# Hybrid encoder step on one core: the S5 lift set between its gates, the SSD beside the other gates

## Chip, cores and metric

One core of a Trainium2 chip runs the whole program. The metric is the device time of one execution in microseconds (us). The engines are called PE (TensorE, with its weight loads PEld), DVE (VectorE), ACT (ScalarE), POOL (GpSimd) and SP (SyncE, which issues every DMA of this kernel).

## What is computed

One layer of a hybrid encoder on 592 rows (16 meta tokens, 512 prompt rows, 64 sample rows) of width 1024. All is float32.

```
h = rmsnorm(x)
p = h @ w_in                       # columns z, xbc, dt, u, q, k, v, gates
y_a = groupnorm(ssd(xbc, dt) * silu(z))         # Mamba-2 scan in chunks
y_b = s5(u)                                     # complex diagonal scan
glu = gelu(y_b) @ w_glu
out_b = glu[:, :1024] * sigmoid(glu[:, 1024:])
o_c = stick_breaking(q, k, v)                   # with a cache of 512 rows
g0, g1, g2 = sigmoid(h @ w_gate)                # three gates of width 1024
mix = g0*(y_a @ w_lift_a) + g1*out_b + g2*(o_c @ w_lift_c)
x = x + mix @ w_out
x = x + relu(rmsnorm(x) @ w_up)**2 @ w_down
```

## The kernel before

Everything is kept transposed, channels on partitions, rows along the free axis. Each weight block of 128x1024 numbers is a *unit*; `units` (L71) lists them in the order in which they are loaded and used: u, then q, v and k, then `mixed()` (L62: ten xbc, eight z, then the gates g1, g2, g0 with eight units each), then eight glu, four lc, eight la, eight out, and the MLP. A float32 product is made of three passes: weights and operands are split into a high and a low part (`split`, L252, ACT writes the high, DVE the low part), and `mm3` (L331) issues hi*hi, hi*lo and lo*hi for each block of 128 rows of the contraction.

`dense` (L379) runs one unit over two halves of the columns (288 each). A half of a gate unit is 24 matmuls (eight blocks); glu and lc contract over 512 channels only, so a half there is 12 matmuls and one unit has two outputs. Each half has one PSUM tile `ps_d` out of three (L190), which is free again when its reader is done. In a glu unit (L1466) ACT turns the second output into `gls` by a sigmoid, DVE multiplies it into the gate `gt`, and DVE multiplies the first output with that into `mix`. In a gate unit (`do_gate`, L552) ACT's sigmoid alone empties the PSUM tile, and the gate goes to DRAM (`g_scr`). A gate is loaded back by `gate_tile` (L1450) into one of three `gt` tiles. For lc, DVE multiplies the output with g2 and POOL adds it to `mix`.

The three branches between the projections are Python generators. After each half, `side` (L373) adds the branch's number in `PACE` (L35) to a credit, and for each whole credit `pull` runs the generator to its next `yield`; so S5, attention and SSD lie between the dense halves, one after the other. `in_order` keeps a pulled piece behind what its engines were given before; a scheduler then fixes each engine's order.

At the end of S5 its output goes to DRAM (`yb_scr`); attention loads it back tile by tile (`s5_load`, L873) and splits it into `ybx` (`s5_split`, L878), one of four tiles in each of its four rounds. The SSD works through six chunks. Behind them `gated` (L1345) multiplies with z and gathers squares in `sa` (part 0 are the first 288 columns, part 1 the others, two channel tiles at a time), `normed` (L1359) sums `sa` over partitions with a matmul by ones (`ps_n`, L408), takes the reciprocal root (`rstd_of`, L240: Ln, Exp and Square on ACT, two steps on DVE) and multiplies four channel tiles of `ya`; `scaled_split` makes `yah` and `yal` for la. Before, part 1 is gated whole, then both groups are normed, each followed by its four splits:

```python
            for m in range(0, 8, 2):
                gated(1, m)
                yield
            for g in range(2):
                normed(1, g)
                yield
                for m in range(4 * g, 4 * g + 4):
                    scaled_split(ya[:, m, on], sg[:, m:m + 1], yah[:, m, on], yal[:, m, on])
```

glu starts behind `until("attn")`, la behind `until("gated")`.

Of the kernel before, what the change touches and what calls it, by code (L numbers as in the profile page):

```python
# [17 lines left out]
T = TP + TS  # L18
# [16 lines left out]
PACE = {"s5_parts": 1.25, "s5": 1.35, "attention": 1.8, "ssd": 1.1}  # L35
# [26 lines left out]
def mixed():  # L62
    n = dict.fromkeys("xzabc", 0)
    out = []
    for c in ORDER:
        out.append(({"x": "xbc", "z": "z", "a": "g1", "b": "g2", "c": "g0"}[c], n[c]))
        n[c] += 1
    return out


def units():  # L71
    u = [("u", m) for m in range(4)] + [(n, m) for m in range(4) for n in ("q", "v", "k")]
    u += mixed()
    u += [("glu", m) for m in range(8)] + [("lc", m) for m in range(4)]
# [102 lines left out]
def body(tc, io):  # L177
# [6 lines left out]
    with ExitStack() as ctx:  # L184
# [303 lines left out]
        oc_scr = dram.tile([8, 128, T], F32, name="oc_scr")  # L488
        g_scr = [dram.tile([8, 128, T], F32, name="g_scr%d" % j) for j in range(3)]
# [62 lines left out]
        def do_gate(j, m):  # L552
            o = etile("go", "ec")
            dense(("g%d" % j, m), hh, hl, lambda cols, ps: sigmoid(ps, o[:, cols]))
            SP.dma_start(g_scr[j][m, :, on], o[:, on])
# [164 lines left out]
        def s5():  # L720
# [150 lines left out]
            yield  # L871

# [12 lines left out]
        def attention():  # L885
# [100 lines left out]
            for t in range(4):  # L986
                (v, vc), (kc, ks, qs) = vv, new
                yb = s5_load(t)
# [139 lines left out]
                s5_split(t, yb)  # L1128
                yield
            a1.release()  # L1130
            ap.release()
            done["attn"] = True
# [71 lines left out]
        def ssd():  # L1204
# [160 lines left out]
            for c in range(1, 6):  # L1365
# [3 lines left out]
                if c == 5:  # L1369
                    normed(0, 0)  # L1370
# [15 lines left out]
                if c == 5:  # L1386
                    normed(0, 1)
# [5 lines left out]
                if c == 4:  # L1393
                    gated(0, 4)
                    gated(0, 6)
                yield
# [7 lines left out]
            for m in range(0, 8, 2):  # L1404
                gated(1, m)
                yield
            for g in range(2):
                normed(1, g)
                yield
                for m in range(4 * g, 4 * g + 4):  # L1410
                    scaled_split(ya[:, m, on], sg[:, m:m + 1], yah[:, m, on], yal[:, m, on])
                    if m % 2:
                        yield
# [16 lines left out]
        pulls.append((attention(), PACE["attention"]))  # L1430
        for n, m in mixed():
# [4 lines left out]
            elif n == "z":  # L1436
                do_z(m)
            else:
                do_gate(int(n[1]), m)

        def until(n):
            while n not in done:
                pull()


        until("s5")
        lp, ybx = late["p"], late["ybx"]
# [8 lines left out]
        ocx = keep.tile([128, 8, T], F32R, name="ocx", tag="hh")  # L1456
        for m in range(8):
            g = gate_tile(1, m)
            s = etile("gls", "ec")

            def ev_b(cols, ps):
                sigmoid(ps, s[:, cols])
# [199 lines left out]
```

## Time and profile before

| | |
|---|---|
| Median of the runs | 1118.86 us (1118.25, 1118.86, 1122.1) |
| Profiled execution, its own time | 1120.97 us |
| Its span | 1119.2 us |
| Mean granted clock, of full speed | 0.994 |
| PE busy, matmuls | 1100.5 us (98%), 8532 |
| PEld busy | 1061.7 us (95%) |
| DVE busy | 794.3 us (71%) |
| ACT busy | 539.6 us (48%) |
| POOL busy | 183.7 us (16%) |
| DMA | 144.04 MB, mean 129 GB/s |

A busy PE isn't a PE at its peak: matmuls overlap, so the number of matmuls in a stretch tells more than its busy time. The stages, from the tiles' first and last instructions: S5 ends at 283 us, the gates run from 291 to 511 us with attention beside them (294 to 482), the SSD from 482 to 584 us, glu from 510 to 598, lc from 598 to 628, la from 628 to 680.

### The profile page before, as it was taken

To read this page: it belongs to the slowest core of one execution; us is meant where nothing else is said; L and a number is where in the kernel's file an instruction comes from. 1 tells how busy PE (TensorE), PEld (TensorE's weight loads), DVE (VectorE), ACT (ScalarE), POOL (GpSimd) and SP (SyncE) were. 2 spreads that over 40 slices of the span, in tenths; PEclk is the share of its full clock that TensorE was granted. 3 is DMA by queue.
4 is the path that set the end of the run, shared out by engine and by line. 5 is a ranking of instruction groups with operands and counts; after the bars stand their busy time and mean duration, and the time that the engine had idled before them with its cause. 6 is when DMAs were issued, how large, how long until landed. Compare 5 with 4: busy or idle time off the path is not lost.

```text
span 1119.2 us, 21309 instructions
## 1 busy us (share of the span) xinstructions
PE 1100.5 (98%) x8532; PEld 1061.7 (95%) x8532; DVE 794.3 (71%) x1377; ACT 539.6 (48%) x896; POOL 183.7 (16%) x240
## 2 busy tenths in 40 slices
PE   9999999999999999999998999999999999999998
PEld 8998999999998999898788999999999999999998
DVE  7968579955667475549988754467866785786787
ACT  6455465523365455465668323355444444444443
POOL 2086256611000000005422300300000000000000
PEclk9999999989999999999999999999999999999999
DMA  7663224466754353277445543322232223223222
GB/s 275 147 145 115 84 90 125 110 165 165 241 177 138 113 179 133 89 255 257 129 146 167 151 134 99 99 75 94 76 102 88 75 77 115 74 76 129 79 81 80
DMA packets 80594, 144.04 MB, mean 129 GB/s; under 512 B 26512, under 2 KB 40688, under 8 KB 79984
## 3 DMA queue, kind: packets, MB, share of 16 engines
q1 hardware_dynamic: 80496, 142.69, 41.0%
q8 instruction: 67, 1.10, 0.4%
q14 instruction: 31, 0.25, 0.1%
HBM read 117.40 MB, written 24.38 MB: 127 GB/s over the span
## 4 chain that ended last, share of the span: by engine, by line
PE 80%; DVE 10%; POOL 3%; ACT 2%; DMA 2%; issue 2%; SPq 1%; DVEq 0%; ACTq 0%; POOLq 0%
PE ps_d L336 18%; PE ps_d L337 18%; PE ps_d L338 18%; PE ps_x L1581 3%; PE ps_x L1580 3%; PE ps_x L1582 3%; PE ps_o L895 2%; PE ps_z L895 2%; PE ps_y L1581 1%; PE ps_y L1580 1%; PE ps_y L1582 1%; DVE w_lo L217 1%; DVE ar L1272 1%; DVE ar L217 1%; POOL cm L217 1%
## 5 line engine op out<-in xcount | busy, mean ns | idle before, releaser
L336 PE MATMUL ps_d<-hh,w_hi 128*128 128x288 f32 (+1 forms) x864 | 260.5, 301 | 0.0
L338 PE MATMUL ps_d<-hh,w_lo 128*128 128x288 f32 (+1 forms) x864 | 260.0, 301 | 0.0
L337 PE MATMUL ps_d<-hl,w_hi 128*128 128x288 f32 (+1 forms) x864 | 260.0, 301 | 0.0
L253 ACT ACTIVATE w_hi<-w_raw 128x1024 fp32r<-128x1024 f32 (+1 forms) x150 | 151.8, 1012 | 220.7 <-PE ps_d L337 142.8
L217 DVE TENSOR_TENSOR w_lo<-w_raw,w_hi 128x1024 fp32r<-128x1024 f32 (+1 forms) x150 | 179.2, 1195 | 104.2 <-ACT w_hi L253 103.7
L337 PEld LDWEIGHTS ps_d<-hl,w_hi 128*128 128x128 f32 x864 | 164.5, 190 | 0.9 <-issue 0.3
L338 PEld LDWEIGHTS ps_d<-hh,w_lo 128*128 128x128 f32 x864 | 164.7, 191 | 0.5
L336 PEld LDWEIGHTS ps_d<-hh,w_hi 128*128 128x128 f32 x864 | 164.7, 191 | 0.4
L336 PE MATMUL ps_d<-x2h,w_hi 128*128 128x288 f32 x512 | 151.3, 296 | 0.0
L337 PE MATMUL ps_d<-x2l,w_hi 128*128 128x288 f32 x512 | 151.1, 295 | 0.0
L338 PE MATMUL ps_d<-x2h,w_lo 128*128 128x288 f32 x512 | 150.3, 295 | 0.0
L338 PEld LDWEIGHTS ps_d<-x2h,w_lo 128*128 128x128 f32 x512 | 96.2, 188 | 0.1
L336 PEld LDWEIGHTS ps_d<-x2h,w_hi 128*128 128x128 f32 x512 | 96.2, 188 | 0.1
L337 PEld LDWEIGHTS ps_d<-x2l,w_hi 128*128 128x128 f32 x512 | 96.2, 188 | 0.0
L253 ACT ACTIVATE w_hi<-ws 128x1024 fp32r<-128x1024 f32 x32 | 34.0, 1061 | 55.0 <-PE ps_y L1581 21.7
L1581 PE MATMUL ps_x<-ftl,w_hi 128*128 128x288 f32 x192 | 56.7, 295 | 0.5 <-DVE ftl L217 0.5
L1580 PE MATMUL ps_x<-fth,w_hi 128*128 128x288 f32 x192 | 56.8, 296 | 0.2 <-ACT s L1600 0.2
L1582 PE MATMUL ps_x<-fth,w_lo 128*128 128x288 f32 x192 | 56.4, 294 | 0.0
L1531 ACT ACTIVATE fr<-ps_d 128x288 f32<-128x288 f32 x64 | 25.7, 402 | 55.8 <-PE ps_d L338 55.8
L217 POOL TENSOR_TENSOR xe<-xd,tend 128x1024 f32<-128x1024 f32 (+2 forms) x6 | 11.6, 1942 | 234.4 <-DVE xd L217 210.1
L217 DVE TENSOR_TENSOR w_lo<-ws,w_hi 128x1024 fp32r<-128x1024 f32 x32 | 39.0, 1220 | 12.6 <-ACT w_hi L253 12.6
L906 DVE TENSOR_TENSOR_SCAN aw<-col,aw 128x400 f32<-128x400 f32 (+4 forms) x36 | 30.7, 899 | 17.3 <-ACT aw L250 17.2
(472 smaller groups left out, 2727.1 us busy)
## 6 DMA issues: line engine op xcount, KB each, us to landing
w_raw<-wts SPq DMA_DIRECT2D x150, 512.0 KB, 3.5
g_scr<-go SPq DMA_DIRECT2D x24, 288.0 KB, 2.8
gt<-g_scr SPq DMA_DIRECT2D x24, 288.0 KB, 3.1
ar<-ac_scr SPq DMA_DIRECT2D x4, 1024.0 KB, 7.2
x_scr<-cs SPq DMA_DIRECT2D x10, 297.5 KB, 2.9
xc<-x_scr SPq DMA_DIRECT2D x4, 640.0 KB, 7.0
xt<-xT SPq DMA_DIRECT2D x8, 296.0 KB, 5.7
z_scr<-zs SPq DMA_DIRECT2D x8, 288.0 KB, 4.6
```

What stands on the lines that cost most here:

```text
L217: e.tensor_tensor(o, a, b, op=op)
L253: S.activation(hi, x, AF.Copy)
L336: PE.matmul(ps, wh[:, c], xh[:, k, cols], start=start and k == 0, stop=False)
L337: PE.matmul(ps, wh[:, c], xl[:, k, cols], start=False, stop=False)
L338: PE.matmul(ps, wl[:, c], xh[:, k, cols], start=False, stop=stop and k == kt - 1)
L895: mm = lambda *a, **b: PE.matmul(*a, skip_group_check=True, **b)
L906: V.tensor_tensor_scan(x, one.to_broadcast([128, n]), x, 1.0, op0=OP.mult, op1=OP.mult)
L1272: V.tensor_scalar(ar[:n, h, :n], ar[:n, h, :n], acm[:n, c, h:h + 1], 0.0, op0=OP.subtract, op1=OP.min)
L1531: S.activation(r[:, cols], ps, AF.Relu)
L1580: PE.matmul(ps, w[0][:, o], fh[:, k], start=first and k == 0, stop=False, skip_group_check=True)
L1581: PE.matmul(ps, w[0][:, o], fl[:, k], start=False, stop=False, skip_group_check=True)
L1582: PE.matmul(ps, w[1][:, o], fh[:, k], start=False, stop=k == 3, skip_group_check=True)
```

## The change

The eight glu units stand between the g1 gates (g1 0, glu 0, g1 1, ...). The g1 gate stays in its SBUF tile, is multiplied there, and the product goes to DRAM (`m_scr`) in the place of the gate; it is loaded into `mix` before lc uses it. `ybx` is needed for that before g1 starts, so S5's own generator loads and splits it, and the main loop pulls until that is done. The attention's output `ocx` takes `ybx`'s place and is loaded when attention ends. g2 and g0 follow, with the SSD's number in `PACE` at 1.25 in place of 1.1. In the SSD's tail the steps of part 0 move by one, and part 1 goes gated 0, 2, 4, normed 0, gated 6, two pieces of splits, normed 1, two pieces of splits.

```diff
--- before.py
+++ after.py
@@ -32,7 +32,7 @@
 LEAD = 120
 WARM = 14
 SPLITS = 3
-PACE = {"s5_parts": 1.25, "s5": 1.35, "attention": 1.8, "ssd": 1.1}
+PACE = {"s5_parts": 1.25, "s5": 1.35, "attention": 1.8, "ssd": 1.25}
 BUFS = {"ea": 3, "eb": 4, "ec": 3}
 
@@ -64,6 +64,8 @@
     out = []
     for c in ORDER:
         out.append(({"x": "xbc", "z": "z", "a": "g1", "b": "g2", "c": "g0"}[c], n[c]))
+        if c == "a":
+            out.append(("glu", n[c]))
         n[c] += 1
     return out
 
@@ -71,7 +73,7 @@
 def units():
     u = [("u", m) for m in range(4)] + [(n, m) for m in range(4) for n in ("q", "v", "k")]
     u += mixed()
-    u += [("glu", m) for m in range(8)] + [("lc", m) for m in range(4)]
+    u += [("lc", m) for m in range(4)]
     u += [("la", m) for m in range(8)] + [("out", m) for m in range(8)]
 
     up = [[("up", 8 * b + 4 * j + k) for k in range(4) for j in range(2)] for b in range(4)]
@@ -486,6 +488,7 @@
         yb_scr = dram.tile([512, 8 * NY], F32, name="yb_scr")
         ya_scr = dram.tile([8, 128, T], F32, name="ya_scr")
         oc_scr = dram.tile([8, 128, T], F32, name="oc_scr")
+        m_scr = dram.tile([8, 128, T], F32, name="m_scr")
         g_scr = [dram.tile([8, 128, T], F32, name="g_scr%d" % j) for j in range(3)]
         ac_scr = dram.tile([96, 128], F32, name="ac_scr")
 
@@ -552,7 +555,24 @@
         def do_gate(j, m):
             o = etile("go", "ec")
             dense(("g%d" % j, m), hh, hl, lambda cols, ps: sigmoid(ps, o[:, cols]))
-            SP.dma_start(g_scr[j][m, :, on], o[:, on])
+            if j != 1:
+                SP.dma_start(g_scr[j][m, :, on], o[:, on])
+            return o
+
+        def do_glu(m, g):
+
+            ybx = late["ybx"]
+            s = etile("gls", "ec")
+
+            def ev_b(cols, ps):
+                sigmoid(ps, s[:, cols])
+                tt(V, g[:, cols], g[:, cols], s[:, cols], OP.mult)
+
+            def ev_a(cols, ps):
+                tt(V, g[:, cols], ps, g[:, cols], OP.mult)
+            w = dense(("glu", m), ybx[:, 0:4], ybx[:, 4:8], ev_b, kt=4, base=4)
+            dense(None, ybx[:, 0:4], ybx[:, 4:8], ev_a, kt=4, base=0, w=w)
+            SP.dma_start(m_scr[m, :, on], g[:, on])
 
         def do_xbc(m):
             pre = etile("pre", "ea", XW)
@@ -869,6 +889,12 @@
             late["dt"] = tc.alloc_tile_pool(name="dtp", bufs=1)
             done["s5"] = True
             yield
+            for m in range(4):
+                x = s5_load(m)
+                yield
+                s5_split(m, x)
+            done["ybx"] = True
+            yield
 
         def s5_load(m):
             x = late["p"].tile([128, T], F32, name="ybl", tag="gt%d" % (m % 3))[:, :8 * NY]
@@ -985,7 +1011,6 @@
             yield
             for t in range(4):
                 (v, vc), (kc, ks, qs) = vv, new
-                yb = s5_load(t)
                 q2, kh, kl = [], [], []
                 for h in range(2):
                     kd, qd = kq[h]
@@ -1125,10 +1150,12 @@
                 split(po[:, 0:TS], och[:, 512:], ocl[:, 512:])
                 SP.dma_start(oc_scr[t, :, on], och.bitcast(F32))
                 SP.dma_start(oc_scr[4 + t, :, on], ocl.bitcast(F32))
-                s5_split(t, yb)
                 yield
             a1.release()
             ap.release()
+            late["ocx"] = ocx = late["p"].tile([128, 8, T], F32R, name="ocx", tag="ybx")
+            for j in range(8):
+                SP.dma_start(ocx[:, j, on].bitcast(F32), oc_scr[j, :, on])
             done["attn"] = True
 
 
@@ -1366,8 +1393,6 @@
                 if c < 5:
                     turned(c + 1)
                 weigh(c)
-                if c == 5:
-                    normed(0, 0)
                 yield
                 if c < 5:
                     decay(c + 1)
@@ -1384,7 +1409,7 @@
                 else:
                     st = sn
                 if c == 5:
-                    normed(0, 1)
+                    normed(0, 0)
                 fetch_chunk(c + 2)
                 yield
                 if c < 5:
@@ -1393,6 +1418,8 @@
                 if c == 4:
                     gated(0, 4)
                     gated(0, 6)
+                if c == 5:
+                    normed(0, 1)
                 yield
             SP.dma_start(io["ssd_out"][1], st)
             d2.release()
@@ -1401,16 +1428,14 @@
             late["l2"] = l2 = tc.alloc_tile_pool(name="late2", bufs=1)
             late["yah"] = yah = l2.tile([128, 8, T], F32R, name="yah", tag="yah")
             late["yal"] = yal = l2.tile([128, 8, T], F32R, name="yal", tag="yal")
-            for m in range(0, 8, 2):
-                gated(1, m)
-                yield
-            for g in range(2):
-                normed(1, g)
-                yield
-                for m in range(4 * g, 4 * g + 4):
+            def parted(m0):
+                for m in range(m0, m0 + 2):
                     scaled_split(ya[:, m, on], sg[:, m:m + 1], yah[:, m, on], yal[:, m, on])
-                    if m % 2:
-                        yield
+
+            for f, x in ((gated, (1, 0)), (gated, (1, 2)), (gated, (1, 4)), (normed, (1, 0)), (gated, (1, 6)),
+                         (parted, (0,)), (parted, (2,)), (normed, (1, 1)), (parted, (4,)), (parted, (6,))):
+                f(*x)
+                yield
             done["gated"] = True
 
 
@@ -1428,6 +1453,10 @@
             do_v(m)
             do_qk("k", m, kg, io["k_out"], halves)
         pulls.append((attention(), PACE["attention"]))
+        def until(n):
+            while n not in done:
+                pull()
+
         for n, m in mixed():
             if n == "xbc":
                 do_xbc(m)
@@ -1435,16 +1464,17 @@
                     pulls.append((ssd(), PACE["ssd"]))
             elif n == "z":
                 do_z(m)
+            elif n == "g1":
+                if m == 0:
+                    until("ybx")
+                g1 = do_gate(1, m)
+            elif n == "glu":
+                do_glu(m, g1)
             else:
                 do_gate(int(n[1]), m)
 
-        def until(n):
-            while n not in done:
-                pull()
-
-
-        until("s5")
-        lp, ybx = late["p"], late["ybx"]
+
+        lp = late["p"]
         mix = keep.tile([128, 8, T], F32, name="mix", tag="hl")
 
         def gate_tile(j, m):
@@ -1453,27 +1483,13 @@
             return g
 
         until("attn")
-        ocx = keep.tile([128, 8, T], F32R, name="ocx", tag="hh")
-        for m in range(8):
-            g = gate_tile(1, m)
-            s = etile("gls", "ec")
-
-            def ev_b(cols, ps):
-                sigmoid(ps, s[:, cols])
-                tt(V, g[:, cols], g[:, cols], s[:, cols], OP.mult)
-
-            def ev_a(cols, ps):
-                tt(V, mix[:, m, cols], ps, g[:, cols], OP.mult)
-            w = dense(("glu", m), ybx[:, 0:4], ybx[:, 4:8], ev_b, kt=4, base=4)
-            dense(None, ybx[:, 0:4], ybx[:, 4:8], ev_a, kt=4, base=0, w=w)
-            if m >= 4:
-                for j in (m - 4, m):
-                    SP.dma_start(ocx[:, j, on].bitcast(F32), oc_scr[j, :, on])
+        ocx = late["ocx"]
         for m2 in range(4):
             w = None
             for j in range(2):
                 m = 2 * m2 + j
                 g = gate_tile(2, m)
+                SP.dma_start(mix[:, m, on], m_scr[m, :, on])
 
                 def ev_c(cols, ps):
                     tt(V, g[:, cols], ps, g[:, cols], OP.mult)
```

How the instructions stand on three places. First ACT at the end of S5; `gsq` is S5's last activation, `zs` a z unit's sigmoid, `go` that of a gate, `ybx<-ybl` the split of S5's output. Before:

```order
L855 ACTIVATE gsq<-ps_y_3234 128x292
L250 ACTIVATE gsq<-gsq 128x292
L253 ACTIVATE w_hi<-w_raw 128x1024
L250 ACTIVATE zs<-ps_d 128x288 x2
L253 ACTIVATE w_hi<-w_raw 128x1024
L250 ACTIVATE zs<-ps_d 128x288
L250 ACTIVATE go<-ps_d 128x288
L253 ACTIVATE w_hi<-w_raw 128x1024
L250 ACTIVATE go<-ps_d 128x288
```

After the change, from the third of the four loads on:

```order
L255 ACTIVATE ybx<-ybl 128x512
L255 ACTIVATE ybx<-ybl 128x64
L252 ACTIVATE zs<-ps_d 128x288
L255 ACTIVATE w_hi<-w_raw 128x1024
L252 ACTIVATE zs<-ps_d 128x288
L255 ACTIVATE ybx<-ybl 128x512
L255 ACTIVATE ybx<-ybl 128x64
L252 ACTIVATE go<-ps_d 128x288
L255 ACTIVATE w_hi<-w_raw 128x1024
L252 ACTIVATE go<-ps_d 128x288
L252 ACTIVATE gls<-ps_d 128x288 x2
```

The splits stand ahead of the first g1 gate, the fourth directly, and two sigmoids of glu 0 follow that gate.

Second, PE where lc (`ocx`) ends and la (`yah`, `yal`) starts. Before, the last `ps_n` stands inside lc, 132 matmuls ahead of la, here:

```order
L337 MATMUL ps_d_7510<-ocx_6889,w_hi_7368 128x288
L338 MATMUL ps_d_7510<-ocx_6889,w_lo_7369 128x288
L408 MATMUL ps_n_6807<-sa_5576,ones_89 128x288
L336 MATMUL ps_d_7524<-ocx_6889,w_hi_7368 128x288
L337 MATMUL ps_d_7524<-ocx_6889,w_hi_7368 128x288
L338 MATMUL ps_d_7524<-ocx_6889,w_lo_7369 128x288
```

and the passage to la is plain:

```order
L336 MATMUL ps_d_7691<-ocx_6889,w_hi_7504 128x288
L337 MATMUL ps_d_7691<-ocx_6889,w_hi_7504 128x288
L338 MATMUL ps_d_7691<-ocx_6889,w_lo_7505 128x288
L336 MATMUL ps_d_7716<-yah_6567,w_hi_7572 128x288
L337 MATMUL ps_d_7716<-yal_6568,w_hi_7572 128x288
L338 MATMUL ps_d_7716<-yah_6567,w_lo_7573 128x288
L336 MATMUL ps_d_7716<-yah_6567,w_hi_7572 128x288
```

After the change the last `ps_n` stands between the two:

```order
L338 MATMUL ps_d_7684<-ocx_5417,w_hi_7492 128x288
L339 MATMUL ps_d_7684<-ocx_5417,w_hi_7492 128x288
L340 MATMUL ps_d_7684<-ocx_5417,w_lo_7493 128x288
L410 MATMUL ps_n_6891<-sa_5702,ones_89 128x288
L338 MATMUL ps_d_7709<-yah_6651,w_hi_7562 128x288
L339 MATMUL ps_d_7709<-yal_6652,w_hi_7562 128x288
```

and three halves of la (ps_d_7709, 7735, 7772) first take their four blocks of channel tiles 0 to 3, 36 matmuls in all, and then tile 4 in turns:

```order
L339 MATMUL ps_d_7772<-yal_6652,w_hi_7632 128x288
L340 MATMUL ps_d_7772<-yah_6651,w_lo_7633 128x288
L338 MATMUL ps_d_7709<-yah_6651,w_hi_7562 128x288
L338 MATMUL ps_d_7735<-yah_6651,w_hi_7562 128x288
L338 MATMUL ps_d_7772<-yah_6651,w_hi_7632 128x288
L339 MATMUL ps_d_7709<-yal_6652,w_hi_7562 128x288
L340 MATMUL ps_d_7709<-yah_6651,w_lo_7563 128x288
```

The last norm moved from inside lc to its end, and la no longer runs half by half at its start.

Third, ACT in the tail of the norm. Before:

```order
L253 ACTIVATE w_hi<-w_raw 128x1024
L257 ACTIVATE yah<-ya,sg 128x576 x4
L243 ACT_TABLE_LOAD
L243 ACTIVATE rsl<-ps_n,col 128x288
L244 ACT_TABLE_LOAD
L244 ACTIVATE sa<-rsl 128x288
L245 ACTIVATE rsl<-sa 128x288
L253 ACTIVATE w_hi<-w_raw 128x1024
L257 ACTIVATE yah<-ya,sg 128x576 x4
L253 ACTIVATE w_hi<-w_raw 128x1024 x3
```

After the change:

```order
L259 ACTIVATE yah<-ya,sg 128x576 x4
L1383 ACTIVATE zl<-ya 128x288
L255 ACTIVATE w_hi<-w_raw 128x1024
L1383 ACTIVATE zl<-ya 128x288
L255 ACTIVATE w_hi<-w_raw 128x1024
L245 ACT_TABLE_LOAD
L245 ACTIVATE rsl<-ps_n,col 128x288
L246 ACT_TABLE_LOAD
L246 ACTIVATE sa<-rsl 128x288
L247 ACTIVATE rsl<-sa 128x288
L259 ACTIVATE yah<-ya,sg 128x576 x4
L255 ACTIVATE w_hi<-w_raw 128x1024
```

Two squares (`zl`) of part 1 and two weight splits now stand between the first four splits and the last norm, and the last four splits directly behind it.

## Rows read from the trace of the kernel before

**Rows 1.** Stretch: us; PE, PEld, DVE, ACT, POOL busy (count); clock, DMA, GB/s.
```profile
294.00:482.00 188.00, 188.00 (x1572) 175.75 (x1572) 112.91 (x179) 98.24 (x189) 0.00 (x0) 1.00 0.46 147
...
511.00:598.00 87.00, 82.34 (x766) 68.24 (x766) 78.71 (x171) 57.10 (x75) 25.00 (x14) 1.00 0.57 174
598.00:628.00 30.00, 27.57 (x197) 26.23 (x196) 28.73 (x49) 18.78 (x27) 11.88 (x7) 1.00 0.56 177
628.00:680.00 52.00, 52.00 (x393) 52.00 (x393) 27.29 (x41) 14.18 (x16) 3.56 (x2) 1.00 0.44 132
```

**Rows 2.** PE's waits, 482 to 632 us: total, times, longest.
```profile
PE ps_d L336 <- DVE mix L217: 2.1, 2, 1.7
PE ps_d L336 <- ACT gls L250: 1.3, 2, 1.1
PE ps_d L336 <- ACT sa L244: 1.3, 1, 1.3
PE ps_y L1318 <- DVE ar L217: 1.2, 2, 0.7
PE ps_d L336 <- DVE gt L217: 1.1, 1, 1.1
```

**Rows 3.** Waits of the weight loads (PEld), the same stretch.
```profile
PEld ps_d L336 <- DVE mix L217: 2.5, 2, 2.0
...
PEld ps_d L336 <- ACT gls L250: 2.0, 3, 1.4
```

**Rows 4.** VectorE groups, 511 to 598 us: busy, mean ns, idle before.
```profile
L217 DVE TENSOR_TENSOR gt<-gt,gls 128x288 f32<-128x288 f32 x14 | 6.3, 464 | 1.6 <-ACT gls L250 1.6
L217 DVE TENSOR_TENSOR mix<-ps_d,gt 128x288 f32<-128x288 f32 x14 | 6.1, 447 | 0.7 <-PE ps_d L338 0.7
```

**Rows 5.** Timeline, ScalarE, last norm: start, us, line, tiles.
```profile
610.64 0.50 ACT L243 ACTIVATE rsl<-ps_n,col 128x288 f32<-128x288 f32 x1
611.16 1.28 ACT L244 ACT_TABLE_LOAD   x1
...
612.93 0.45 ACT L245 ACTIVATE rsl<-sa 128x288 f32<-128x288 f32 x1
```

**Rows 6.** Timeline, VectorE, last two norms and their splits.
```profile
605.27 0.46 DVE L247 SCALAR_TENSOR_TENSOR sa<-rsl,sa 128x288 f32<-128x288 f32 x1
...
606.01 1.56 DVE L217 TENSOR_TENSOR ya<-ya,sa 128x288 f32<-128x288 f32 x4
...
615.84 1.68 DVE L247 SCALAR_TENSOR_TENSOR sa<-rsl,sa 128x288 f32<-128x288 f32 x1
...
618.18 2.78 DVE L217 TENSOR_TENSOR ya<-ya,sa 128x288 f32<-128x288 f32 x4
...
621.25 1.53 DVE L258 SCALAR_TENSOR_TENSOR yal<-ya,sg,yah 128x576 fp32r<-128x576 f32 x2
```

**Rows 7.** Instructions of the tile ps_n: min/median/max ns, first and last start.
```profile
L408 PE MATMUL ps_n<-sa,ones x8: 405/406/407, 576.8 to 606.5; 128*128 128x288 f32 x8
```

**Rows 8.** Timeline, GpSimd, around the end of lc.
```profile
627.72 3.84 POOL L217 TENSOR_TENSOR mix<-mix,gt 128x576 f32<-128x576 f32 x2 [2.56 <-DVE gt L217]
```

**Rows 9.** Timeline, ScalarE, first g1 gate.
```profile
294.56 0.41 ACT L250 ACTIVATE go<-ps_d 128x288 f32<-128x288 f32 x1 [1.96 <-PE ps_d L338]
```

**Rows 10.** Timeline, SyncE queue, the end of the S5 branch.
```profile
287.66 1.64 SPq L587 DMA_DIRECT2D z_scr<-zs  x1
```

**Rows 11.** Loads and splits of yb: min/median/max ns; landing us.
```profile
L253 ACT ACTIVATE ybx<-ybl x8: 304/743/1182, 359.0 to 479.2; 128x512 fp32r<-128x512 f32 x4, 128x64 fp32r<-128x64 f32 x4
...
DMA to landing us min/median/max: 3.0/3.5/4.0
```

**Rows 12.** DMA issues: count, KB each, median us to landing.
```profile
gt<-g_scr SPq DMA_DIRECT2D x24, 288.0 KB, 3.1
```

**Rows 13.** Busy time by stretch, columns as Rows 1.
```profile
226.00:228.40 2.40, 0.03 (x1) 0.00 (x0) 2.40 (x4) 0.70 (x1) 0.95 (x1) 0.99 0.49 131
228.40:238.60 10.20, 10.16 (x44) 10.19 (x45) 4.29 (x9) 1.98 (x5) 2.86 (x2) 0.50 0.73 204
```

More of the change, by code (lines that the diff above doesn't have):

```diff
@@ L1403, in ssd @@
             late["yal"] = yal = l2.tile([128, 8, T], F32R, name="yal", tag="yal")
-            for m in range(0, 8, 2):
-                gated(1, m)
-                yield
-            for g in range(2):
-                normed(1, g)
-                yield
-                for m in range(4 * g, 4 * g + 4):
-                    scaled_split(ya[:, m, on], sg[:, m:m + 1], yah[:, m, on], yal[:, m, on])
-                    if m % 2:
-                        yield
+            def parted(m0):
+                for m in range(m0, m0 + 2):
+                    scaled_split(ya[:, m, on], sg[:, m:m + 1], yah[:, m, on], yal[:, m, on])
+            for f, x in ((gated, (1, 0)), (gated, (1, 2)), (gated, (1, 4)), (normed, (1, 0)), (gated, (1, 6)),
+                         (parted, (0,)), (parted, (2,)), (normed, (1, 1)), (parted, (4,)), (parted, (6,))):
+                f(*x)
+                yield
             done["gated"] = True
```

## Prediction

> **What bounds the kernel now.** I began with busy time by stretch, because the change shifts work between stages. What bounds is PE: with attention beside the gates it is busy for 188.00 of 188.00 us, and in la 393 matmuls fill 52.00 us, which makes a matmul of 288 columns worth 52.00 / 393 = 0.132 us [rows 1]. A matmul that is only put elsewhere therefore saves nothing; the change can win only what PE loses between matmuls. That is little: PE is idle for 87.00 - 82.34 = 4.7 us beside glu and 30.00 - 27.57 = 2.4 us beside lc, and for nothing in the other stages [rows 1]. The view of PE's waits names it. Of 482 to 632 us, 2.1 us went to DVE's `mix` and 1.3 to ACT's `gls` (both empty a glu tile), 1.2 to the SSD's `ar`, and in lc 1.3 to `sa` (ACT's norm steps ahead of something PE needed) and 1.1 to `gt`, 7.0 us in all [rows 2]. The weight loads, which run ahead of the matmuls, waited 2.5 and 2.0 us for the two glu readers [rows 3], so the true price of those two lies between 3.4 and 4.5 us. The reason is DVE: it is busy for 78.71 of 87.00 us in the glu stretch, 90%, and 113 of 188 (60%) where attention runs [rows 1].
>
> **GLU leaves the SSD.** In the stretch 511 to 598 us DVE loses 14 products `gt` of 0.464 us and 14 `mix` of 0.447, 6.3 + 6.1 = 12.4 us [rows 4]; it falls from 78.7 to 66.3 us of 87, or 76%. What stands there instead are g2 and g0 halves, which ACT alone empties, as it did beside attention without a wait of PE. I take the two GLU waits as gone, at the mean of their two views: (3.4 + 4.5) / 2 = -4.0 us. The wait for `ar` is DVE being late in the SSD itself; with DVE less full I take half of it: -0.6. Together **-4.6**, between -3.4 (matmul view, `ar` unchanged) and -5.7 (weight loads' view, `ar` gone).
>
> **GLU beside attention.** 16 pairs of those products cost 16 x 0.911 = 14.6 us of DVE, and the eight splits of `ybx` (some 8 x 0.7 us) leave; 113 us becomes about 122 of 188, 65%. A glu half now lasts 12 x 0.132 = 1.6 us, where a gate half lasts 3.2, and two of its three PSUM tiles wait for DVE behind attention's long instructions. In rows of before such halves cost 3.4 us at 90% DVE and nothing was lost at 60% (with ACT readers): nearer to the second, **+0.5**, ends 0 and +3.5.
>
> **lc.** Its DVE products, POOL additions and loads stay, and the norm of part 1's second group still runs behind it. The waits for `sa` and `gt`, 2.4 us [rows 2], are left: **0**, ends -2.4 (the `sa` wait came from steps that now lie behind lc) and +2.4 (DVE is as full, and part 0's norms are later).
>
> **The start of la.** The faster pace does not bring the norm forward: the order has the last `ps_n` behind the last lc matmul, where it stood 132 matmuls (17 us) ahead of la. PE then has 36 matmuls on channel tiles 0 to 3, and three on tile 4's high part, before it needs `yal` of tile 4: 39 x 0.132 = 5.2 us of cover. The chain over that time: ACT's Ln, table load, Exp and Square, from 610.64 to 612.93 + 0.45 = 613.38, 2.7 us [rows 5]; on DVE two steps of the reciprocal root, the four products `ya` and the first `yal`. In the first group, with POOL idle, a step took 0.46 and four products 1.56; in the second, a step 1.68 and four products 2.78; two `yal` took 1.53 there in between [rows 6], one 0.8, or 1.4 when stretched like the products. Ahead of it all stands the sum's matmul, 0.4 us [rows 7]. So DVE needs 0.9 + 1.6 + 0.8 = 3.3 or 0.5 + 1.7 + 2.8 + 1.4 = 6.4 us, the chain 6.4 or 9.5, and the wait is 1.2 or 4.3 us. Which, rests on POOL: its last two additions to `mix` ran from 627.72 for 3.84 us, that is until 3.6 us past the end of lc at 628 [rows 8], and the chain's DVE part begins 0.4 + 2.7 = 3.1 us past it. They overlap for half a microsecond, so I stand near the fast end: **+2.0**, ends 1.2 and 4.3. Queued behind it are only the further blocks of the same three halves.
>
> The Trainium skill (GPSIMD Engine Reference, section 1, Specifications) states that POOL shares its SBUF interfaces with VectorE, and that an instruction of VectorE with two SBUF inputs contends for them. The rows agree that such DVE instructions have two durations, 1.56 and 2.78; taken for the whole chain, since lc's additions have just been issued, the rule would give 4.3 at la's start and a sum 2.3 us higher; taken by where POOL's additions end, 1.2 to 2.0.
>
> **The end of S5.** g1 0 is followed at once by glu 0, which reads `ybx`. The first g1 half ended on PE at 294.56 [rows 9], so glu 0 could start 24 x 0.132 = 3.2 us later, at 297.7, and its low part of channel block 3 is wanted 9 matmuls on, at 298.9. Before `ybl` can be loaded, SP issues the last `yb_scr` stores and a `z_scr` store that ends at 287.66 + 1.64 = 289.3 [rows 10]; the load lands in 3.0 to 4.0 us, and a split takes up to 1.18 us on ACT and as much on DVE [rows 11]: 289.3 + 4.0 + 2.4 = 295.7. The four loads are on one queue and have three `gt` buffers, so the fourth waits for a split; 3.2 us are left for that. **0**, ends 0 and +3. SP has no more behind this than weights, which are loaded ahead.
>
> **DMA.** Eight stores and eight loads of `m_scr` take the place of `g_scr1`'s, each 288 KB and landed in 3.1 us [rows 12]. The `mix` loads wait on SP for the last reader of `hl` (the last g0 half) with lc's and the tail's loads behind them; lc's first addition comes a unit later. **0**. Reordering part 0's norms moves them by one piece, no instruction more: **0**.
>
> **The sum.** -4.6 + 0.5 + 0 + 2.0 + 0 = -2.1 us. The profiled execution took 1120.97 us, so it would take 1118.9; the median of the runs is 1118.86, which gives **1116.8 us**. The part of the claim that PE waits less beside the SSD comes true, and half of it is given back where the last norm now stands. A measurement of this kernel can tell 0.5%, 5.6 us, from no change: faster is below 1113.3, slower above 1124.5.
>
> **Rivals.**
> *A, slower: la's wait costs the clock too.* At 226 us PE did nothing for 2.40 us, and for the next 10.2 us the granted clock was 0.50, the lower of the two levels, 1.2 GHz [rows 13]: 5.1 us lost. If the norm's chain runs as slowly as it did in lc (Ln at 610.64, first `yal` of the group done at 621.25 + 0.77 = 622.0, 11.4 us, and 0.4 for the sum) the wait is 11.8 - 5.2 = 6.6 us in one piece. Then 1118.86 - 4.6 + 0.5 + 6.6 + 5.1 = 1126.5. It decides from some 2.4 us of wait. For it: my slow end is 4.3. Against it: the lc work that stretched the chain is over, and the wait at 592 us of 1.7 us [rows 2] left the clock at 1.00 in that stretch [rows 1].
> The Trainium skill (TensorE: Matmul & The Clock Gate, section HAM oscillation) describes a matmul run that waits for DMA and starts again throttled. By it the price of a long wait is the wait and a stretch of half clock behind it; the trace agrees at 226, and shows none behind the wait at 592.
> *B, faster: DVE was the whole cause.* All of the GLU waits by the weight loads' view (4.5), all of `ar` (1.2) and lc's 2.4 go, beside attention none come, and la waits 1.2: -8.1 + 1.2 = -6.9, 1112.0. For it: all waits of 482 to 632 stand beside a DVE at 90% or more; against it: lc's DVE work hardly changes.
> *C: `ybx` is late.* The fourth split takes its buffer 3 us too late: 1119.8, no change.
> *D: GLU's waits only move.* Beside attention they return whole, +3.5 for 0.5: 1119.8, no change, and slower (1124.9) only with the half clock as well.
>
> **Chances.** Forecast 0.43, A 0.23, B 0.22, C 0.05, D 0.07. B alone lies below 1113.3, but only just, so some of it counts as no change, which the low tail of the forecast makes up: faster 0.24. A alone lies above 1124.5: slower 0.23. The rest, 0.53, is no change. The likeliest case's own range is 1113 to 1120; the range takes in B whole (its other 3.6 us stretched as the weight loads' view stretches GLU's, 4.5 for 3.4, would be 1.2 more, and the fastest of the runs shown is 0.6 below the median: 1110.2) and A: 1110.2 to 1126.5.
>
> **What would show it.** Right: no wait of PE for `gls` or `mix` between 482 and 598; a wait of PE or PEld for `yal` or `yah` of 1 to 3 us once lc has ended, at the granted clock 1.00; PE full from 294 to 482; the first glu matmul straight behind the first g1 unit. A is right if la's first 10 us show the clock 0.50, B if neither lc nor la waits, C if PE waits for `ybx` at 298, D if waits for `gt` or `gls` appear during attention. The forecast is wrong if the stretch with the SSD is no shorter per matmul than it was.

## Result and the profile after

The change made the kernel slower: 1135.39 us (median of six executions, 1132.05 to 1138.42) against 1118.67, a ratio of 1.0141, interval [1.0123, 1.0158], or +16.7 us where -2.1 was forecast. The profiled execution took 1135.48 us with a span of 1133.4 (1119.2 before).

The stages first, with columns as in [rows 1]; lc now runs from 599.9 to 637.2 us and la from there to 693.2. Three short stretches behind waits follow.

```profile
294.00:482.00 188.00, 188.00 (x1550) 173.69 (x1549) 121.94 (x231) 93.71 (x180) 0.00 (x0) 1.00 0.44 138
...
482.00:599.90 117.90, 112.93 (x978) 97.50 (x977) 85.18 (x159) 72.72 (x89) 34.86 (x18) 0.97 0.54 173
599.90:637.20 37.30, 28.98 (x198) 27.67 (x197) 29.11 (x50) 18.54 (x28) 11.68 (x7) 0.95 0.65 213
637.20:693.20 56.00, 53.48 (x387) 52.72 (x386) 32.37 (x48) 19.80 (x24) 1.43 (x1) 0.97 0.40 119
...
517.00:522.00 5.00, 4.74 (x20) 4.74 (x21) 5.00 (x11) 4.10 (x3) 0.00 (x0) 0.50 0.46 116
...
607.00:612.00 5.00, 5.00 (x28) 5.00 (x28) 3.23 (x9) 1.67 (x4) 1.41 (x1) 0.66 0.95 330
...
646.00:650.00 4.00, 4.00 (x23) 4.00 (x22) 1.58 (x3) 0.36 (x1) 0.00 (x0) 0.66 0.00 0
```

In the attention stretch PE is busy throughout, as before, though DVE's busy time there rose from 112.9 to 121.9 us. But the 188 us now hold 1550 matmuls where they held 1572 [rows 1], with attention's own all there both times: 22 projection matmuls less, 22 x 0.132 = 2.9 us. No wait of PE shows there, and what costs this time was not traced. The larger loss is later: lc takes 37.3 us where it took some 30, la 56.0 where it took 51 or 52 [rows 1]. PE's waits from 500 to 650 us (total, times, longest) name it:

```profile
PE ps_x L1279 <- DVE cb L219: 5.0, 1, 5.0
PE ps_d L338 <- DVE gt L219: 4.7, 3, 1.9
PE ps_d L338 <- ACT go L252: 3.6, 1, 3.6
PE ps_d L338 <- ACT yah L259: 2.1, 1, 2.1
PE ps_d L339 <- DVE yal L260: 0.4, 1, 0.4
```

The waits for `gls` and `mix` of [rows 2] are gone, as forecast. In their place stand 15.8 us where 7.0 were, and behind three of them the granted clock was low: 0.50 from 517 to 522, 0.66 from 607 to 612 and again from 646 to 650. What that costs is (1 - clock) x time, 2.5 + 1.7 + 1.4 us, and some 0.6 in the stretches beside them: about 6 us. So 8.8 + 6 us of waits and clock, and the 3 us beside attention, stand against the span's 14.2 and 2.6 us by which the first glu unit started earlier in this execution (at 294.9 us; before, as many matmuls had run at 297.6).

The same by stage, from the times at which equally many matmuls had run in both traces: the change is 2.6 us ahead when its first glu unit starts, 0.4 behind at the end of attention, 2.1 behind when lc starts, 9.3 when la starts and 14.2 when la ends. Attention costs 3.0 us, the SSD beside the other gates 1.7 (a wait for `cb` with its clock, less the saved GLU waits), lc 7.2 and la 4.9. So the stretch with the SSD is no shorter (978 matmuls in 117.9 us; from 482 to 598 before, 977 in 116.0), which the prediction named as the sign that it is wrong.

**The wait of 5.0 us (the SSD's start).** DVE, then POOL, from 506 to 518 us (start, length, line, tiles, count):

```profile
506.61 1.06 DVE L1299 TENSOR_SCALAR ar<-ar,acm 128x128 f32<-128x128 f32 x5
...
508.19 8.82 DVE L1299 TENSOR_SCALAR ar<-ar,acm 128x128 f32<-128x128 f32 x6
516.93 0.28 DVE L219 TENSOR_TENSOR cb<-ps_bt,cst 128x128 f32<-128x128 f32 x1
```

```profile
508.42 2.01 POOL L219 TENSOR_TENSOR xe<-xd,tend 128x1024 f32<-128x1024 f32 x1 [13.04 <-DVE xd L219]
510.39 2.38 POOL L219 TENSOR_TENSOR a<-a,xc 128x1024 f32<-128x1024 f32 x1
512.74 1.89 POOL L219 TENSOR_TENSOR ya<-xc,pa 128x1024 f32<-128x1024 f32 x1
514.59 2.33 POOL L219 TENSOR_TENSOR a<-a,xc 128x1024 f32<-128x1024 f32 x1
```

Five steps of a decay take 1.06 us; the next six take 8.82, and end as POOL ends. Four of the six fill that time, 1.93, 2.43, 1.93 and 2.37 us long, beside POOL's products of 2.01, 2.38, 1.89 and 2.33. The decays of two chunks stand together, 32 such steps, and the `cb` that frees a PSUM tile for PE stands behind most of them. Such a step is not new: before, one took 2.48 us at 530.0. PE then waited for nothing from 527 to 542 us. So the place of such a step counts, and what stands behind it.

**The wait of 3.6 us (the start of lc).** ScalarE from 592 to 607 us:

```profile
596.64 1.28 ACT L245 ACT_TABLE_LOAD   x1
597.94 0.50 ACT L245 ACTIVATE rsl<-ps_n,col 128x288 f32<-128x288 f32 x1
598.46 1.28 ACT L252 ACT_TABLE_LOAD   x1
599.75 0.41 ACT L252 ACTIVATE go<-ps_d 128x288 f32<-128x288 f32 x1
600.18 1.28 ACT L246 ACT_TABLE_LOAD   x1
...
603.28 0.44 ACT L1381 ACTIVATE sa<-ya 128x288 f32<-128x288 f32 x1 [0.89 <-DVE ya L219]
...
605.02 1.28 ACT L252 ACT_TABLE_LOAD   x1
606.32 0.41 ACT L252 ACTIVATE go<-ps_d 128x288 f32<-128x288 f32 x1
```

The gates' last matmul ran at 599.7, but the sigmoid that empties its tile only at 606.32: the norm's Ln and Exp of part 0, a table load between any two functions, an activation that waits for DVE and a weight split stand ahead of it. PE fills the two tiles it has and stops.

**The wait of 2.1 + 0.4 us (the start of la).** ScalarE, then DVE's products:

```profile
638.05 1.28 ACT L245 ACT_TABLE_LOAD   x1
639.35 0.50 ACT L245 ACTIVATE rsl<-ps_n,col 128x288 f32<-128x288 f32 x1
639.87 1.28 ACT L246 ACT_TABLE_LOAD   x1
...
643.59 2.77 ACT L259 ACTIVATE yah<-ya,sg 128x576 fp32r<-128x576 f32 x4 [1.51 <-DVE ya L219]
```

```profile
643.10 1.56 DVE L219 TENSOR_TENSOR ya<-ya,sa 128x288 f32<-128x288 f32 x4
```

PE is out of matmuls on channel tiles 0 to 3 some 0.3 us past 642.03, where the last of them starts, and needs the first `yah` of the second group, which starts behind the first of the four products.

**The waits for `gt`** in lc are three, of 1.0, 1.9 and 1.8 us. Behind the second DVE had stood idle for 2.37 us, until 620.27, for ScalarE's part of a norm's root, with the product of a lifted half queued behind that step. The other two were not taken apart.

### The profile page after: what moved, and what is told of

Its sections match the earlier page's. It is cut to its first block, busy times and chain, and to the rows that moved or that the text cites. A ratio compares the mean times of both kernels' runs of the same rounds, so it can differ in the third digit from the quotient of the medians.

```text
span 1133.4 us, 21299 instructions
## 1 busy us (share of the span) xinstructions
PE 1105.6 (98%) x8532; PEld 1065.1 (94%) x8532; DVE 800.9 (71%) x1377; ACT 543.4 (48%) x898; POOL 179.9 (16%) x240
## 4 chain that ended last, share of the span: by engine, by line
PE 80%; DVE 7%; DMA 4%; POOL 3%; ACT 3%; SPq 2%; issue 1%; DVEq 0%; ACTq 0%; POOLq 0%
PE ps_d L338 18%; PE ps_d L340 18%; PE ps_d L339 18%; PE ps_x L1597 3%; PE ps_x L1596 3%; PE ps_x L1598 3%; PE ps_o L921 2%; PE ps_z L921 2%; PE ps_y L1597 1%; PE ps_y L1596 1%; PE ps_y L1598 1%; PE ps_y L1345 1%; DVE w_lo L219 1%; DMA tz<-kd_scr 1%; DVE ar L1299 1%
## 5 line engine op out<-in xcount | busy, mean ns | idle before, releaser
L219 DVE TENSOR_TENSOR w_lo<-w_raw,w_hi 128x1024 fp32r<-128x1024 f32 (+1 forms) x150 | 181.7, 1212 | 103.0 <-ACT w_hi L255 100.7
```

The costliest lines, as they stand in the source:

```text
L219: e.tensor_tensor(o, a, b, op=op)
```

## Experiments

Medians in us; the ratio is to the kernel before on the same chip, whose medians lie between 1118.67 and 1119.47. In the rows, "new norms" is the change's order of the norm steps, and "no root" leaves out the reciprocal root of the SSD's norms.

| | median | ratio, interval |
|---|---|---|
| the change | 1135.39 | 1.0141 [1.0123, 1.0158] |
| e1: GLU's move alone | 1130.93 | 1.0098 [1.0081, 1.0115] |
| e2: GLU's move, pace 1.25 | 1128.74 | 1.0091 [1.0066, 1.0116] |
| f2: GLU's move, new norms | 1127.30 | 1.0081 [1.0055, 1.0108] |
| e6: before, pace 1.25 | 1133.43 | 1.0116 [1.0096, 1.0136] |
| e7: before, new norms | 1121.48 | 1.0015 [1.0001, 1.0028] |
| e3: before, both | 1127.01 | 1.0072 [1.0051, 1.0093] |
| e4: the change, ocx loads later | 1136.94 | 1.0148 [1.0128, 1.0168] |
| e5: the change, less work on POOL | 1128.79 | 1.0080 [1.0060, 1.0100] |
| e8: e1, the SSD earlier | 1132.18 | 1.0102 [1.0080, 1.0124] |
| e9: the change, no root | 1124.62 | 1.0048 [1.0031, 1.0066] |
| e10: e1, no root | 1123.59 | 1.0040 [1.0022, 1.0058] |
| f1: before, no root | 1115.98 | 0.9968 [0.9956, 0.9980] |
| e11: e1, mix loaded in turn | 1130.22 | 1.0094 [1.0075, 1.0114] |
| f3: e1, one activation for two | 1124.08 | 1.0042 [1.0026, 1.0058] |
| e12: before, one activation for two | 1117.18 | 0.9978 [0.9966, 0.9989] |

### The parts of the change, one by one

e1 takes the change's pace and norm order back:

```diff
-PACE = {..., "ssd": 1.25}
+PACE = {..., "ssd": 1.1}
-                         (gated, (1, 4)), (normed, (1, 0)), (gated, (1, 6)),
...
+            for m in range(0, 8, 2):
+                gated(1, m)
...
```

> The change without its SSD part: pace 1.1 and the norm steps in their old order; GLU, ybx, ocx and m_scr as in the change. Theory N (norm order): the waits for go (3.6), gt (4.7), yah and yal (2.5) and the half clock behind two of them (1.8 each) come from the new order of the norm steps, and go; what is left is the wait for cb of 5.0 us with its half clock (3.4): about 1135.4 - 14.4 + 2.4 (the lc waits of before) = 1123. Theory G (GLU's move): the SSD has lost the glu units that it ran beside, so its tail meets lc and la in whatever order the norms stand: 1132 or more, with waits of 8 us or more between 590 and 650.

e2 takes back the norm order alone:

> The change with the norm steps in their old order and the pace left at 1.25. Theory N: no wait for go above 1.5 us, no wait of la, about 1123, the same as without the whole SSD part. Theory G: 1132 or more. A third, P (pace): the wait for cb at 512 us stands because the faster pace puts two chunks' decays together; then this one still has it and the run without the pace does not, and they differ by 8 us.

e3 puts pace and norm order on the kernel before:

> The kernel before with the change's SSD part alone (pace 1.25, norm steps in their new order), GLU left where it was. Theory N: the norm order costs without GLU's move too, in lc and at la's start: 1118.7 + 6 to 10 = 1125 to 1129. Theory G: the order itself costs little, 1118 to 1121. Theory P: a wait of PE behind the decays at 505 to 520 us, + 5 to 8.

All three are slower than before by 0.7 to 1.0%. Theory N fails: e1 and e2 should have come to 1123. G comes within 1.1 us in e1 (1130.93 for 1132 or more), but not in e2 (1128.74), so it doesn't hold alone either. Undoing the norm order wins 6.7 us on the change, not 12. P is borne out in the wait: the run at pace 1.1 waits 1.9 us for `cb`, the one at 1.25, with the same norms, 5.1. It is not borne out in the time: the two were to differ by 8 us, and the one with the wait is 2.2 us faster, within the noise of the two (1.0091 and 1.0098). e3's 1127.0 lies where N and P both had it, but its long wait is one of 6.2 us for `gls`, and neither had that. PE's waits of GLU's move alone (e1, 482 to 650 us):

```profile
PE ps_d L338 <- ACT go L252: 2.6, 2, 2.1
PE ps_d L338 <- DVE gt L219: 2.5, 3, 1.8
PE ps_n L410 <- DVE sa L219: 2.5, 2, 1.3
PE ps_x L1279 <- DVE cb L219: 1.9, 1, 1.9
```

e6 and e7 split what e3 had joined: `"ssd": 1.25` alone, and the norm order alone, each on the kernel before.

> The kernel before with the SSD's pace at 1.25 and nothing else. The SSD part cost 7.7 us there, with one wait for gls of 6.2 us behind a decay that met POOL. Theory P (pace): the pace alone does it, 1124 to 1128, with a wait of 3 us or more behind a decay. Theory N (norm order): 1118 to 1121.

> The kernel before with the norm steps in their new order and the pace left at 1.1. Theory N: 1124 to 1128; the order has its last norm 13 matmuls ahead of la (133 before), so a wait of la as in the change, 2 us with half clock or more. Theory P: 1118 to 1121.

P, though above the 1124 to 1128 that it expected: the pace alone costs 14.4 us, the norm order 2.5 (1.0015, far below half a per cent). With both the loss is 7.7, so the parts don't add. Where the pace's loss is, the largest of PE's waits of e6 (500 to 650 us) shows, with its ScalarE, DVE and POOL at the longest:

```profile
PE ps_d L336 <- ACT gls L250: 9.8, 3, 5.5
```

```profile
569.81 1.28 ACT L1273 ACT_TABLE_LOAD   x1 [3.25 <-DVE ar L1272]
...
573.80 0.41 ACT L250 ACTIVATE gls<-ps_d 128x288 f32<-128x288 f32 x1
```

```profile
563.12 5.52 DVE L1272 TENSOR_SCALAR ar<-ar,acm 64x64 f32<-64x64 f32 x13 [0.33 <-ACT a L1270]
```

```profile
563.29 1.90 POOL L217 TENSOR_TENSOR ya<-xc,pa 128x1024 f32<-128x1024 f32 x1
565.25 0.95 POOL L1275 MEMSET ar<- 64x1024 f32 x1
```

Thirteen steps of a decay take 5.52 us on DVE while POOL works until 567.6, ScalarE's Exp waits for them, and the sigmoid that would free PE's tile stands behind that Exp. It looks like the change's mechanism, at another place; no run took POOL's work out here.

f2 leaves the norms new and takes the pace back to 1.1 in the change:

> The change with the pace back at 1.1, all else as in the change (1135.4). Theory P with C: the two decays no longer meet in one queue behind POOL, the cb wait falls from 5.0 to 2 us and loses its half clock, as in GLU's move alone: 1135.4 - 3 - 3.4 = 1129. If the pace is only dear beside glu units (where ScalarE and VectorE both empty tiles): 1134 or more.

The pace costs 8 us in the change too; `cb` waits 2.4 us in two pieces, and the clock stays at 1.00 behind it.

With these runs all eight ways to join the three parts are measured, and none has a price of its own. By the medians, the pace costs 14.4 us on the kernel before, 5.5 with the new norms (e7 to e3), 8.1 with GLU moved and the new norms (f2 to the change), and nothing with GLU moved and the old norms (e1 to e2, -2.2). The norm order costs 2.5 before and 6.7 with both other parts, but wins 6.4 at pace 1.25 (e6 to e3) and 3.6 with GLU moved (e1 to f2). GLU's move costs 11.7 alone, 5.8 with the new norms (e7 to f2) and 8.4 with both (e3 to the change), but wins 4.7 at pace 1.25 (e6 to e2). What a part does hangs on the order of the queues that it meets.

### POOL and the decays

```diff
-                tt(G, a2[:, :, :n], a2[:, :, :n], xc[:, 9, :n].unsqueeze(1).to_broadcast([128, 8, n]), OP.mult)
```

> The change without the SSD's POOL product a<-a,xc (five instructions of 1.3 to 3.3 us; the off-diagonal part of the SSD's output is then not weighted by C, so the output is not the reference's). The order on DVE and PE is that of the change. Theory C (contention): six tensor-scalar steps of a decay took 8.8 us on DVE while POOL worked from 508 to 517, where others take 0.25 us each, and cb waits behind them; with less of POOL's work there they take some 4 us, the cb wait of 5.0 us falls to about 1 and its half clock (3.4) goes: 1135.4 - 7.4 = 1128. If the decays are late for another reason (ar loaded late, table loads on ACT): cb still waits for 4 us or more, 1134 to 1137.

1128.79, and `cb` waits 0.9 us. The same six steps and POOL beside them, in e5:

```profile
508.28 4.56 DVE L1299 TENSOR_SCALAR ar<-ar,acm 128x128 f32<-128x128 f32 x6
```

```profile
508.50 2.01 POOL L219 TENSOR_TENSOR xe<-xd,tend 128x1024 f32<-128x1024 f32 x1 [13.03 <-DVE xd L219]
510.48 1.90 POOL L219 TENSOR_TENSOR ya<-xc,pa 128x1024 f32<-128x1024 f32 x1
```

They start at the same time and again last about as long as POOL works, now to 512.4 rather than 516.9, and the granted clock from 512 to 522 is 1.00. Theory C is shown for the wait for `cb`: from the end of attention to the start of lc this execution takes 5.4 us less than the change's, and 6.6 is what the median gains. (lc is 2.6 us longer in it, at a clock of 0.50 from 600 to 606, and the edit leaves out five of POOL's products, so not all of the 6.6 need be this one meeting.) The Trainium skill (SBUF — State Buffer, section Who interferes with whom) has a rule for it: an instruction of VectorE in a two-port mode and one of GpSimd contend for a shared pair of ports, which the first to issue holds to its end while the other is fully blocked, and a tensor-scalar can enter such a mode. The trace agrees in the lengths, a single step up to 2.43 us long beside POOL's products of up to 2.38; whether these steps run in that mode it doesn't show.

### The loads of ocx and of mix

e4 issues the `ocx` loads ahead of lc in the program:

```diff
-            for j in range(8):
-                SP.dma_start(ocx[:, j, on].bitcast(F32), oc_scr[j, :, on])
...
         ocx = late["ocx"]
+        for j in range(8):
+            SP.dma_start(ocx[:, j, on].bitcast(F32), oc_scr[j, :, on])
```

> The change with the eight ocx loads issued where lc starts and no longer at the end of attention, ahead of the SSD's first loads. Theory O: they hold back the queue (its last two were issued at 485.8, 3.4 us behind the last store) and so the SSD's first ar; decays of two chunks then meet, and the wait for cb (5.0) and its half clock (3.4) are due to them: 1135.4 - 8.4 = 1127. If the cb wait has another cause: 1134 to 1137, cb wait still near 5 us.

Nothing changed (`cb` waits 4.9 us), but the run says little: the order of the queue is the scheduler's, and of the last two loads one stayed at 487.9 us, ahead of the SSD's first `ar`, and the other went to 493.8. That these loads are not the cause is borne out by e1 rather, which keeps them where the change has them and waits 1.9 us.

e11 loads the products into the idle `gls` tiles in turn:

```diff
-                SP.dma_start(mix[:, m, on], m_scr[m, :, on])
+                s = etile("gls", "ec")
+                SP.dma_start(s[:, on], m_scr[m, :, on])
...
-                tt(G, mix[:, m, on], mix[:, m, on], g[:, on], OP.add)
+                tt(G, mix[:, m, on], s[:, on], g[:, on], OP.add)
```

> GLU's move alone with the products loaded into the three gls tiles in turn (free by then) and added from there into mix, so that no load waits for the last reader of hl and they don't come in one burst (DMA share 0.95 to 1.03 from 606 to 620 us in the change). Theory M: lc, 36.7 us long, falls to 32 or less, 1126. Theory T: unchanged, 1129 to 1132.

1130.22 and lc 37.6 us long: the loads of `mix` don't matter. Theory M falls.

### The SSD earlier

`"attention": 1.9` in e1.

> GLU's move without the SSD part (pace 1.1, old norm order) and attention's pace at 1.9 in place of 1.8, by which the SSD starts 91 matmuls (12 us) earlier; last norm 184 matmuls ahead of la in place of 92. Theory L (late): GLU's move costs 11.7 us because the SSD's tail meets lc; then this takes back most of it, 1117 to 1123, lc 30 to 32 us long in place of 36.7. Theory G (the SSD runs worse beside gates than beside glu, wherever it lies): 1127 or more, with waits for go and cb before lc.

1132.18: the SSD started at 481 us where it had started at 492, and nothing was won. lc took 35 us; PE waited 1.6 us for `go`, 1.6 for `sa`, 3.6 for `gt`, and in the SSD itself 4.1 us for `ar`. Theory L falls: how early the tail lies is not what decides.

### The norm's chain on ScalarE

```diff
-                rstd_of(p, ps[:, :n], size, out[:, cols], n, "rs")
+                l = p.tile([128, 296], F32, name="rsl", tag="rsl")[:, :n]
+                V.tensor_scalar(l, ps[:, :n], size * EPS, None, op0=OP.add)
+                V.tensor_scalar(out[:, cols], l, -2.0, None, op0=OP.mult)
```

> The change with the reciprocal root of the SSD's four norms left out (ScalarE's Ln, Exp and Square with their table loads; two VectorE steps of the same length stay, so the products are scaled wrongly). Theory T (tables): the waits for go (3.6), for yah and yal (2.5) and the half clocks behind them (1.8 each) come from table loads and from activations that wait for VectorE, ahead of a gate's sigmoid: 1135.4 - 9.7 = 1125 or 1126, with the cb wait of 5 us still there. If the norms' place (their VectorE steps) is the cause: 1131 or more.

> The same left out of GLU's move alone (pace 1.1, old norm order; 1130.9). Theory T: what GLU's move costs is that gates, which only ScalarE empties, now run up to lc where glu's tiles were emptied by VectorE; the waits for go (2.6) with the half clock at 620 (1.7) and some of those for sa (2.5) go: 1124 to 1126. Theory M (the loads of mix): 1129 or more.

> The kernel before with the reciprocal root of the SSD's norms left out as in the two runs above (ScalarE's three activations and their table loads; the products are scaled wrongly). Theory T says that the chain hurts where gates run up to lc: before it costs little, 1115 to 1118, against 7.3 us with GLU moved and 10.8 in the change. If it costs as much before (1112 or less), the chain is dear everywhere, and GLU's move costs its 11.7 us for another reason.

Without the chain the change is 10.8 us faster, GLU's move 7.3, the kernel before 3.5. In e9 the waits for `go`, `yah` and `yal` are gone, la takes 51 us again and `cb` still waits 3.9 us. ScalarE at the start of lc in e10, and PE's waits of e10 from 500 to 650 us:

```profile
591.16 0.39 ACT L252 ACTIVATE go<-ps_d 128x288 f32<-128x288 f32 x1
...
595.41 0.39 ACT L252 ACTIVATE go<-ps_d 128x288 f32<-128x288 f32 x1
```

```profile
PE ps_d L338 <- DVE gt L219: 2.7, 3, 1.5
PE ps_x L1281 <- DVE cb L219: 1.6, 1, 1.6
PE ps_y L1347 <- DVE ar L219: 1.2, 2, 0.8
```

Each sigmoid runs when its tile is full, no load between, and lc is back at 30.9 us. Theory T is shown for the start of lc: the chain ahead of the sigmoid is the cause. At la's start no sigmoid waits; there the chain itself is what PE waits for, and it is shorter. f1 came out as T had it: the chain is dearest where the gates run up to lc and the last norm up to la. These runs take out table loads and activations together, so the loads' own share isn't shown.

In f3 and e12 nothing is left out:

```diff
-                rstd_of(p, ps[:, :n], size, out[:, cols], n, "rs")
+                l = p.tile([128, 296], F32, name="rsl", tag="rsl")[:, :n]
+                y = out[:, cols]
+                S.activation(y, ps[:, :n], AF.Abs_reciprocal_sqrt, scale=1.0 / size, bias=eps)
+                S.activation(l, y, AF.Square)
+                V.scalar_tensor_tensor(l, ps[:, :n], size * EPS, l, op0=OP.add, op1=OP.mult)
+                V.scalar_tensor_tensor(y, l, -3.0 * size, y, op0=OP.add, op1=OP.mult)
```

> GLU's move alone with one activation (reciprocal square root) in place of Ln and Exp in the SSD's norms, nothing left out. Theory T: half of the table loads are left, so half of the 7.3 us comes back: 1130.9 - 3.6 = 1127. If only a chain without any table load helps: 1130 or more.

> The kernel before with the reciprocal root of the SSD's norms seeded by one activation (reciprocal square root) in place of Ln and Exp: one table load and one activation less for each of four norms, 1.7 us shorter each. Theory T: part of the waits for gls (1.3) and sa (1.3) goes: 1116.5 to 1118. Without T: 1118 to 1120.

f3 wins 6.9 us on GLU's move, more than the half that was expected. e12 is the fastest whole version: 0.9978, interval [0.9966, 0.9989], so faster than both kernels, though by less than the half per cent that the prediction asked for.

## Why the prediction was wrong

- **Part right: "GLU leaves the SSD" (-4.6).** The two GLU waits went. The step failed in its next sentence, that ScalarE alone empties g2 and g0 halves "as it did beside attention without a wait of PE". Beside the SSD ScalarE also has the norms' Ln and Exp and the decays' Exp, with table loads between, and PE waited 3.6 us for `go`. I costed the readers that left, and not the queue of the reader that came. Taking the norm's chain out of that queue is worth 10.8 us in the change (e9) and 7.3 in GLU's move alone (e10), against 3.5 in the kernel before (f1).
- **Wrong: the pace.** I asked only whether it brings the last norm forward, and gave it no term. Alone it costs 14.4 us on the kernel before (e6), 8 in the change (f2), though nothing with GLU moved and the old norms (e2 against e1). The traces name the place: pieces offered sooner put decays together, beside POOL's products and ahead of readers of PSUM. e5 shows that for the change; for e6 it is read from the trace alone.
- **Wrong: "Reordering part 0's norms ... 0" and "lc: 0".** On the kernel before the reordering costs 2.5 us, on the change (against e2) 6.7, and in two other settings it wins. In lc the waits went from 2.4 us (`sa` 1.3, `gt` 1.1) to 8.3 (`go` 3.6, `gt` 4.7), where my upper end allowed 4.8; with the clock the stage lost 7.2 us.
- **Half right, and partly by luck: the start of la.** Of wait +2.0 was forecast and 2.1 + 0.4 measured, but the stage lost 4.9 us, above the upper end of 4.3, because the clock, forecast at 1.00, fell: 0.66 from 646 to 650. The size of the wait came out of errors that nearly cancel: the chain was summed with one table load where there are two (1.28 us each), and with all four products ahead of the split where it needed one (1.56 us for the four). The condition set for rival A's clock, some 2.4 us of wait, did not hold either: it fell behind 2.1 here and stayed up behind 2.6 in f2. Rival A had the side and this part of the mechanism, with a chance of 0.23, but placed all of its loss at la, where 4.9 of 14.2 us lie, and reached 1126.5.
- **Right: the end of S5; half right: GLU beside attention.** PE has no wait from 294 to 482 us, none for `ybx`, and DVE's busy time came to 121.9 us where 122 was forecast; rival C is out, and D's waits did not come. But the stretch lost 3.0 us without a wait, where +0.5 was forecast with an upper end of 3.5, so the step's reason, tiles that wait for DVE, was not what cost the time. Rival B fell with the waits in lc.
- **The range** ended at 1126.5 because each bound was taken from waits the trace of before showed. None of its rows had a gate's sigmoid behind a norm's chain, or two decays together, so the ends of these costs were not 0; I left them out rather than bound them.

**What stays open.** In the profiled executions GLU's move without the chain (e10) is 1.7 us slower than the kernel before, counted from the sigmoid of the second g1 half (1116.6 - 294.3 = 822.3 us, before 1119.2 - 298.6 = 820.6; that of the first waits behind a split of `ybx` in e10). Its median, 1123.59, is 4.5 us above its profiled execution (1119.09), and the profiled execution of e1 and e8 is the fastest of theirs as well. The other executions had less clock: e10's profiled one was granted 0.999 on the mean, the nine others 0.990 to 0.996, and the slowest, 1130.97 us, had the lowest. Where in the program it fell was not seen. And against f1, which has no chain either, GLU's move still costs 1.0040 / 0.9968 = 1.0072, some 8 us. So the chain explains 3.8 of its 11.7 us, and the 3.0 us beside attention, which each trace with GLU beside attention at the same pace shows (e10's too), a further part whose cause is open; the rest is not shown.

## What to carry to other kernels

When work is moved off a stretch, price the queue of the engine that empties PSUM in its place: every instruction ahead of that reader counts, with its table loads and with what it waits for itself. A pace that offers side work sooner is an edit with a price of its own; look at what it places ahead of the readers of PSUM, and at which VectorE steps it sets beside GpSimd's. Try the parts of a change one by one, and then in pairs: here each of them alone was slower, their losses did not add, and one part even won in the company of another.

## What was not expected of the hardware

The steps of a decay, some 0.2 us apart when they run freely, took up to 2.43 us beside GpSimd, and the next VectorE instruction starts within 0.4 us of GpSimd's end (516.93 and 516.92 in the change, 512.77 and 512.38 in e5). How long PE waited did not settle whether the clock fell: it did behind the 2.1 us at la's start (0.66 from 646 to 650), and in f2 it stayed at 1.00 behind 2.6 us for `go`. The half clock behind the wait at 226 us comes and goes between executions of the same stretch of S5: 0.74 on average from 225 to 245 us before, 0.91 in the change, 1.00 in e10, worth up to 5 us in a span that all of them share.
